# Retention scores of a pair of heads computed together, with the pass over the queries' lower parts on 64 rows of the matrix unit for each head

## The chip, the core and the metric

The kernel runs on one core of one Trainium2 chip. A core has a matrix unit (TensorE; in profiles PE, and PEld for the loading of its stationary operands), a vector engine (VectorE, DVE), a scalar engine (ScalarE, ACT), a general engine (GpSimd, POOL) and SyncE (SP), which here only issues transfers. Each engine works through its own list of instructions in order and waits on semaphores for the others. 16 DMA engines move data between the chip's memory and the on-chip buffers. The metric is the time of one execution in microseconds (us), taken as the median of several runs.

## The reference

One layer of a streaming encoder on 2048 positions of width 1024: a normalization, one wide input projection, a branch of chunked attention, a branch of retention, gates, two output projections, a merge, a last projection and a last normalization, all in 32-bit floats. The change lies in retention, whose core is this (heads H = 8, key width 64, value width 128, chunks of 64):

```python
s = jnp.einsum('bnqhd,bnkhd->bnhqk', qc, kc) * intra_decay
o_intra = jnp.einsum('bnhqk,bnkhe->bnqhe', s, vc)
kv = jnp.einsum('bnkhd,hk,bnkhe->nbhde', kc, state_decay, vc)
def step(state, kv_n):
    return state * chunk_decay[None, :, None, None] + kv_n, state
_, state_prev = lax.scan(step, jnp.zeros((B, H, dk, dv)), kv)
o_cross = jnp.einsum('bnqhd,nbhde->bnqhe', qc, state_prev) * cross_decay.T[:, :, None]
```

The scores `s` are products of queries and keys over 64 numbers, weighted with a decay.

## The kernel before

**Parts.** To reach 32-bit accuracy, operands are split into an upper part (a rounded copy, made by ScalarE) and a lower part (the rest, made by VectorE or GpSimd), and a product is the sum of the products of parts.

**Stages.** The kernel runs: first half of the positions projected, attention for it, retention for it; the same for the second half; then the merge. Retention, `retention(s, ps_ret)` for s = 0 and 1, works through the four pairs of heads `p`, and in each through four stretches of 256 positions `st` (T = 256), so 16 steps for each half and 32 in all. In each step both heads `i` = 0, 1 of the pair are taken one after the other.

**Filling.** Retention's own matmuls stand between matmuls of a projection (`ps_g_...` in the profile) that are ready at any time: `fill(n)` writes n portions of these, each of three matmuls of 512 columns, into TensorE's order. What other engines do is put off by `later(n, fn)`: `fn` is written when n more portions have been. The order in which the code is written is the order of each engine's list.

**One step before the change.** `load_scored(p, st)` brings keys and queries, written two steps ahead of their use. The tile of keys, `kr`, has 128 rows: on rows 0 to 63 the keys' upper parts for both heads, on rows 64 to 127 their lower parts; two transfers, one for each half of the rows. Each head's tile of queries, `qr`, holds the queries' upper part and, behind it, their lower part, and both once more on the other 64 rows; two transfers for each head. SyncE issues these six one after the other. `scores(p, st, i)` then makes the scores of one head in one accumulator bank (`sr`, two banks) with four matmuls on all 128 rows: for each half `kk` of the keys, the keys' 128 rows with the queries' upper part, and again with their lower part. The bank holds 256 columns for the first half of the keys and 128 for the second, where the decay is zero for the rest. Because upper and lower keys lie on different rows, each pass sums two products of parts; the second pass adds upper keys by lower queries and lower keys by lower queries.

**Behind the scores** VectorE multiplies with the decay mask (`sm`), ScalarE takes the upper part (`sh`), GpSimd the lower (`sl`). `output(p, st, i, ...)` adds, in the only bank `o`, the state's share (`o<-qr,sstk`) and the scores' share (`o<-sh,vr`, `o<-sl,vr`). `evacuate` copies `o` for both heads (ScalarE: `oz`, then the squares), sends `oz` out (SyncE, `ors<-oz`) and sums the squares (`ssq`). `update` adds to the state (`kv`).

**Order of one step.** With n counting heads, the loop writes for each: a fill, `output` of this head, `scores` of the same head of the next step, for the first head `load_scored` of the step after that, and a fill. So the scores of the two heads are half a step apart.

**Buffers.** All these tiles come from one pool of 25 equal buffers; a tile takes a buffer when an earlier one is done with, and its first writer waits for that one's last reader.

In the profile every operation is at line 143, a helper that records it; tiles are told by name.

Of the kernel before, what the change touches and what calls it, by code (L numbers as in the profile page):

```python
# [11 lines left out]
F32 = mybir.dt.float32  # L12
# [9 lines left out]
P = 128  # L22
# [8 lines left out]
T = 256  # L31
# [42 lines left out]
def hybrid_kernel(  # L74
# [30 lines left out]
    def r32(ap):  # L105
        return ap.bitcast(F32)
# [47 lines left out]
    dma = Ordered(nc.sync).dma_start  # L154
# [90 lines left out]
    def later(n, fn):  # L245

        order[0] += 1
        deferred.append((steps[0] + n, order[0], fn, free[0]))
        deferred.sort(key=lambda e: e[:2])
# [86 lines left out]
    class Strassen(Chunk):  # L336
        tag = ""
# [1274 lines left out]
    def retention(s, ps_ret):  # L1612
# [4 lines left out]
        todo = [(p, st) for p in range(4) for st in range(4 * s, 4 * s + 4)]  # L1617
        tiles, values, dms = {}, {}, {}
        begun = [False]

        def load_scored(p, st):
# [5 lines left out]
            qs = []  # L1627
            for n in range(2):
                dma(
                    r32(ks[64 * n:64 * n + 64]),  # L1630
                    r32(krscr[cc][b][un, n, 2 * (p % 2):2 * (p % 2) + 2]).rearrange("i c h t -> (c h) i t"),
                )
            for i in range(2):
# [33 lines left out]

        def scores(p, st, i):

            nm = f"{p}_{st}_{i}"  # L1670
            ks, qs = tiles[p, st]
            sp = ps_ret.tile([P, 512], F32, tag="sr", bufs=2, name=f"sr_{nm}")[:, 0:T + P]
            for kk in range(2):
                o = sp[:, kk * T:T + kk * P]
                kcol = ks[:, i, kk * P:(kk + 1) * P]
                pe.matmul(o, kcol, qs[i][:, 0, kk * P:], start=True, stop=False)
                pe.matmul(o, kcol, qs[i][:, 1, kk * P:], start=False, stop=True)
            got = []
# [14 lines left out]

            later(1, masked)
            return got
# [114 lines left out]
        fill(13)  # L1810
        parts = {items[0]: scores(*items[0])}
        fill(RET_FILL)
        parts[items[1]] = scores(*items[1])
        fill(RET_FILL * 2)
        for n, (p, st, i) in enumerate(items):
# [12 lines left out]
            if i == 1:  # L1828
                pend = evacuate(p, st, ops)
            if n + 2 < len(items):  # L1830
                parts[items[n + 2]] = scores(*items[n + 2])
            if i == 0 and m + 2 < len(todo):
                load_scored(*todo[m + 2])
            fill(RET_FILL)
            if n % 8 in (4, 6) and p < 3:
                load_mask(p + 1, n % 8 // 2 - 2)
        fill(9)
# [204 lines left out]
```

## Time and profile before

| | |
|---|---|
| median of 3 runs | 1908.64 us (1907.68 to 1913.85) |
| the profiled execution's own time | 1909.69 us |
| its span from first to last instruction | 1907.9 us |
| matmuls, loads of stationary operands | 10213 each |
| score matmuls of 256 columns, 128 columns (`sr<-qr,kr`) | 128 of each, busy 29.1 and 21.6 us |
| retention's two stretches | about 565 to 717 us and 1325 to 1480 us |
| transfers of keys and of queries for the scores | 64 of 128 KB, 128 of 128 KB |

Busy times are sums over overlapping instructions and don't add up to the time that they hold up what follows; the distance between the starts of neighbouring instructions does. A row such as `x4` in the order of time merges neighbours of the same kind; its first number is the first one's start, the second the time from there to the last one's end. A bracket at a row's end is the time in which the engine stood still before it, and what ended that. `SPq` and `ACTq` are the queues in which SyncE and ScalarE issue transfers.

### The profile page before, as it was taken

To read this page: it belongs to the slowest core of one execution; us is meant where nothing else is said; L and a number is where in the kernel's file an instruction comes from. 1 tells how busy PE (TensorE), PEld (TensorE's weight loads), DVE (VectorE), ACT (ScalarE), POOL (GpSimd) and SP (SyncE) were. 2 spreads that over 40 slices of the span, in tenths; PEclk is the share of its full clock that TensorE was granted. 3 is DMA by queue.
4 is the path that set the end of the run, shared out by engine and by line. 5 is a ranking of instruction groups with operands and counts; after the bars stand their busy time and mean duration, and the time that the engine had idled before them with its cause. 6 is when DMAs were issued, how large, how long until landed. Compare 5 with 4: busy or idle time off the path is not lost. (4 is left out here: it accounts for less than half of the span.)

```text
span 1907.9 us, 31062 instructions
## 1 busy us (share of the span) xinstructions
PE 1866.9 (98%) x10213; PEld 1604.4 (84%) x10213; DVE 1355.7 (71%) x2456; ACT 933.1 (49%) x1931; POOL 665.3 (35%) x583
## 2 busy tenths in 40 slices
PE   7999999999999999999999999999999999999998
PEld 6899889888888888899889888887888878888886
DVE  6879888677655658889798677765546766767665
ACT  7555554666654455443333666664455321223544
POOL 0102105455645561001105554554564000002775
PEclk9999999999999999999999999999999999999999
DMA  6586976666549987775776656555998999986673
GB/s 197 158 275 200 282 265 213 185 193 185 175 144 278 279 257 258 231 233 195 222 247 202 185 165 180 166 150 155 275 283 265 326 355 345 322 291 227 209 238 127
DMA packets 325553, 435.88 MB, mean 228 GB/s; under 512 B 29880, under 2 KB 191184, under 8 KB 325392
## 3 DMA queue, kind: packets, MB, share of 16 engines
q1 hardware_dynamic: 260096, 368.35, 60.7%
q10 hardware_dynamic: 65296, 65.55, 11.2%
q8 instruction: 81, 1.33, 0.3%
q14 instruction: 80, 0.66, 0.1%
HBM read 288.14 MB, written 145.64 MB: 227 GB/s over the span
## 5 line engine op out<-in xcount | busy, mean ns | idle before, releaser
L143 POOL TENSOR_SCALAR pr<-pr,rsum 128x640 f32<-128x640 f32 (+4 forms) x128 | 100.0, 781 | 197.7 <-DVE rsum L143 130.7
L143 DVE TENSOR_TENSOR ptl<-tp,pth 128x512 fp32r<-128x512 f32 (+1 forms) x168 | 100.3, 597 | 91.7 <-ACT pth L143 77.8
L143 ACT ACTIVATE pr<-pr,mn 128x640 f32<-128x640 f32 (+4 forms) x128 | 97.9, 765 | 123.3 <-DVE mn L143 97.3
L143 PE MATMUL ps_g_x<-r,wh_g 128*128 128x512 f32 x448 | 141.5, 397 | 1.0 <-ACT u_g L143 0.9
L143 PE MATMUL ps_g_z<-r,wh_g 128*128 128x512 f32 x448 | 141.1, 396 | 0.0
L143 POOL TENSOR_TENSOR l_vr<-vrt,h_vr 128x512 fp32r<-128x512 f32 x32 | 47.7, 1492 | 202.4 <-DMA qrs<-l_q 131.6
L143 POOL TENSOR_TENSOR t_out<-raw_out 128x512 f32<-128x512 f32 x7 | 14.1, 2008 | 263.2 <-DVE wl_out L143 263.2
L143 DVE CUSTOM_DVE_ANT_0 pr<-wide,bt 128x640 f32<-128x640 f32 (+4 forms) x128 | 93.7, 732 | 16.5 <-PE wide L143 13.5
L143 ACT CAST pth<-tp 128x512 fp32r<-128x512 f32 (+1 forms) x168 | 85.3, 507 | 38.9 <-PE tp L143 34.2
L143 PE MATMUL wide<-ka,qa 128*128 128x384 f32 (+1 forms) x448 | 94.9, 327 | 2.9 <-DVE mn L143 2.7
L143 DVE TENSOR_TENSOR sm<-sr,dm 128x384 f32<-128x384 f32 x64 | 35.6, 556 | 85.3 <-PE sr L143 33.9
L143 ACT CAST wh_p<-raw_p 128x512 fp32r<-128x512 f32 x111 | 67.9, 618 | 51.0 <-PE ps_p_y L143 18.2
L143 POOL TENSOR_TENSOR sl<-sm,sh 128x384 fp32r<-128x384 f32 x64 | 69.8, 1090 | 64.8 <-ACT sh L143 44.0
L143 PEld LDWEIGHTS tp<-ident,pr 128*128 128x128 f32 x560 | 71.8, 141 | 23.5 <-POOL pr L143 1.0
L143 PEld LDWEIGHTS ps_g_x<-r,wh_g 128*128 128x128 f32 x448 | 79.6, 189 | 13.9 <-ACT u_g L143 2.3
L143 PEld LDWEIGHTS ps_g_z<-r,wh_g 128*128 128x128 f32 x448 | 79.5, 188 | 12.4
L143 PE MATMUL tp<-ident,pr 128*128 128x128 f32 x560 | 89.0, 272 | 0.3
L143 PE MATMUL ps_g_z<-r,wl_g 128*128 128x512 f32 x224 | 88.2, 394 | 0.0
L143 PE MATMUL ps_g_x<-r,wl_g 128*128 128x512 f32 x224 | 88.1, 393 | 0.0
L143 POOL TENSOR_TENSOR wl_g<-t_g,wh_g 128x512 fp32r<-128x512 f32 x56 | 75.5, 1349 | 35.1 <-ACT wh_g L143 33.8
L143 DVE TENSOR_TENSOR wl_p<-raw_p,wh_p 128x512 fp32r<-128x512 f32 x111 | 79.5, 723 | 7.7 <-ACT wh_p L143 5.4
L143 POOL TENSOR_TENSOR t_g<-raw_g,t_g 128x512 f32<-128x512 f32 x56 | 73.8, 1318 | 28.1 <-issue 8.9
(927 smaller groups left out, 6016.7 us busy)
## 6 DMA issues: line engine op xcount, KB each, us to landing
raw_g<-in_w_in_dram ACTq DMA_DIRECT2D x56, 512.0 KB, 4.9
raw_p<-in_w_in_dram ACTq DMA_DIRECT2D x50, 512.0 KB, 5.8
qa<-qas SPq DMA_DIRECT2D x128, 128.0 KB, 3.4
qr<-qrs SPq DMA_DIRECT2D x128, 128.0 KB, 4.8
vr<-vrs SPq DMA_DIRECT2D x64, 256.0 KB, 5.6
ka<-kas SPq DMA_DIRECT2D x56, 256.0 KB, 4.1
va<-vas SPq DMA_DIRECT2D x40, 256.0 KB, 3.4
kds<-kdt_k SPq DMA_DIRECT2D x32, 256.0 KB, 4.8
```

The costliest lines, as they stand in the source:

```text
L143: return tc.keep_in_program_order(op(*a, **k))
```

## The change

Both heads' scores of a step are made in one place, right behind the first head's `output` of the step before; their eight matmuls come in two passes of four. In the first, each head and each half of the keys has a matmul on all 128 rows with the queries' upper part. In the second, each has one with the queries' lower part on 64 rows only: the first head on rows 0 to 63, the second on rows 64 to 127, taking turns. For that, the keys of the second head are loaded the other way round, upper parts on rows 64 to 127, so that the 64 rows used hold upper parts for both heads; the keys come in four transfers of 64 rows by 256 columns. The product of lower keys and lower queries is no longer computed. The second head's mask and split are written one portion after the first head's. Fills stay as many; the masks of the next pair's second head are loaded one head sooner.

```diff
         def load_scored(p, st):
 ...
-            for n in range(2):
-                dma(
-                    r32(ks[64 * n:64 * n + 64]),
-                    r32(krscr[cc][b][un, n, 2 * (p % 2):2 * (p % 2) + 2]).rearrange("i c h t -> (c h) i t"),
-                )
+            for i in range(2):
+                for n in range(2):
+                    at = 64 * (n ^ i)
+                    dma(
+                        r32(ks[at:at + 64, i]),
+                        r32(krscr[cc][b][un, n, 2 * (p % 2) + i]).rearrange("c h t -> (c h) t"),
+                    )
 ...
-        def scores(p, st, i):
+        def scores(p, st):
+
+            ks, qs = tiles[p, st]
+            sps = [ps_ret.tile([P, 512], F32, tag="sr", bufs=2, name=f"sr_{p}_{st}_{i}")[:, 0:T + P] for i in range(2)]
+            todo = [(sps[i][:, kk * T:T + kk * P], i, kk) for kk in range(2) for i in range(2)]
+            for o, i, kk in todo:
+                pe.matmul(o, ks[:, i, kk * P:(kk + 1) * P], qs[i][:, 0, kk * P:], start=not kk, stop=False,
+                          skip_group_check=True)
+            for o, i, kk in todo:
+                hi = slice(64 * i, 64 * i + 64)
+                pe.matmul(o, ks[hi, i, kk * P:(kk + 1) * P], qs[i][hi, 1, kk * P:], start=False, stop=bool(kk),
+                          skip_group_check=True)
+            for i in range(2):
+                parts[p, st, i] = scored(p, st, i, sps[i])
+
+        def scored(p, st, i, sp):
 
             nm = f"{p}_{st}_{i}"
-            ks, qs = tiles[p, st]
-            sp = ps_ret.tile([P, 512], F32, tag="sr", bufs=2, name=f"sr_{nm}")[:, 0:T + P]
-            for kk in range(2):
-                o = sp[:, kk * T:T + kk * P]
-                kcol = ks[:, i, kk * P:(kk + 1) * P]
-                pe.matmul(o, kcol, qs[i][:, 0, kk * P:], start=True, stop=False)
-                pe.matmul(o, kcol, qs[i][:, 1, kk * P:], start=False, stop=True)
 ...
-            later(1, masked)
+            later(1 + i, masked)
 ...
-        parts = {items[0]: scores(*items[0])}
-        fill(RET_FILL)
-        parts[items[1]] = scores(*items[1])
-        fill(RET_FILL * 2)
+        scores(*todo[0])
+        fill(RET_FILL * 3)
 ...
-            if n + 2 < len(items):
-                parts[items[n + 2]] = scores(*items[n + 2])
+            if i == 0 and m + 1 < len(todo):
+                scores(*todo[m + 1])
             if i == 0 and m + 2 < len(todo):
                 load_scored(*todo[m + 2])
             fill(RET_FILL)
-            if n % 8 in (4, 6) and p < 3:
-                load_mask(p + 1, n % 8 // 2 - 2)
+            if n % 8 in (4, 5) and p < 3:
+                load_mask(p + 1, n % 8 - 4)
```

On TensorE, at the first step of the first half (`sr_0_0` and `sr_0_1` are the two heads' banks, in the short form of the names; `qr_0_0`, `qr_0_1` their queries):

```order
 L143 MATMUL ps_g_8_y<-r_88,wl_g_8_1_7065 128x512
-L143 MATMUL sr_0_0_7181<-qr_0_0_7091,kr_0_7088 128x256 x2
-L143 MATMUL sr_0_0_7181<-qr_0_0_7091,kr_0_7088 128x128 x2
+L143 MATMUL sr_0_0_7185<-qr_0_0_7093,kr_0_7088 128x256
+L143 MATMUL sr_0_1_7186<-qr_0_1_7096,kr_0_7088 128x256
+L143 MATMUL sr_0_0_7185<-qr_0_0_7093,kr_0_7088 128x128
+L143 MATMUL sr_0_1_7186<-qr_0_1_7096,kr_0_7088 128x128
+L143 MATMUL sr_0_0_7185<-qr_0_0_7093,kr_0_7088 128x256
+L143 MATMUL sr_0_1_7186<-qr_0_1_7096,kr_0_7088 128x256
+L143 MATMUL sr_0_0_7185<-qr_0_0_7093,kr_0_7088 128x128
+L143 MATMUL sr_0_1_7186<-qr_0_1_7096,kr_0_7088 128x128
```

The head's four matmuls have become the pair's eight, the heads taking turns; the last four are those on 64 rows.

On ScalarE, around the evacuation of the output of the second step of the first pair (`sh_2_0`, `sh_2_1`: upper parts of the third step's scores, first and second head), before:

```order
L143 CAST sh_2_0_7407<-sm_2_0_7396 128x384
L143 ACTIVATE u_g_8_7287<-u_g_8_7287 128x512
L143 DMA raw_g_10_1_7411<-in_w_in_dram 128x4x256
L143 CAST wh_g_9_3_7413<-raw_g_9_1_7125 128x512
L143 COPY oz_1_7436<-o_1_7331 128x512
L143 ACTIVATE o_0_1_7437<-o_1_7331 128x512
L143 CAST o2h_1_7464<-o_0_1_7437 128x512
L143 CAST sh_2_1_7466<-sm_2_1_7440 128x384
```

and after the change:

```order
L143 CAST sh_2_0_7422<-sm_2_0_7409 128x384
L143 ACTIVATE u_g_8_7300<-u_g_8_7300 128x512
L143 DMA raw_g_10_1_7426<-in_w_in_dram 128x4x256
L143 CAST wh_g_9_3_7428<-raw_g_9_1_7129 128x512
L143 CAST sh_2_1_7446<-sm_2_1_7415 128x384
L143 COPY oz_1_7448<-o_1_7341 128x512
L143 ACTIVATE o_0_1_7449<-o_1_7341 128x512
L143 CAST o2h_1_7476<-o_0_1_7449 128x512
```

The second head's cast has moved from behind the squares' cast to the place right ahead of the output's copy.

On SyncE, the loads of the third step, before:

```order
L143 DMA vr_1_1_7238<-vrs_0_213 128x512
L143 DMA kr_2_7269<-krs_1_182 64x2x256 x2
L143 DMA qr_2_0_7272<-qrs_1_190 64x512 x2
L143 DMA qr_2_1_7275<-qrs_1_190 64x512 x2
L143 DMA mas_0_333<-g_0_2_0_7226 128x512
```

and after the change:

```order
L143 DMA vr_1_1_7242<-vrs_0_213 128x512
L143 DMA kr_2_7278<-krs_1_182 64x256 x4
L143 DMA qr_2_0_7283<-qrs_1_190 64x512 x2
L143 DMA qr_2_1_7286<-qrs_1_190 64x512 x2
L143 DMA mas_0_333<-g_0_2_0_7230 128x512
```

Two transfers of keys more stand ahead of the queries.

2 lines of the change are left out of this document (1 added, 1 removed).

## The prediction

> **What bounds the kernel now.** I read the page first, then the two stretches in which retention runs, then TensorE's order of time inside one of them.
>
> ```profile
> span 1907.9 us, 31062 instructions
> PE 1866.9 (98%) x10213; PEld 1604.4 (84%) x10213; DVE 1355.7 (71%) x2456; ACT 933.1 (49%) x1931; POOL 665.3 (35%) x583
> ...
> 565.00:717.00 152.00, 145.48 (x849) 125.41 (x848) 83.61 (x162) 73.28 (x146) 89.56 (x74) 0.99 0.92 269
> ...
> 1325.00:1480.00 155.00, 151.40 (x887) 130.89 (x887) 82.94 (x160) 78.47 (x153) 87.99 (x72) 1.00 0.93 274
> ```
>
> TensorE (PE, with its weight loads PEld) sets the end: 98% of the span. In the two retention stretches (the last two rows: busy time of PE, PEld, DVE, ACT, POOL, then clock, share of the DMA engines, GB/s) it stands still for 6.5 and 3.6 us, and the 16 DMA engines are at 0.92 and 0.93, so memory is a near second there. What the score matmuls cost is not their busy time, since matmuls overlap, but the distance from one start to the next:
>
> ```profile
> 600.12 0.39 PE L143 MATMUL ps_g_y<-r,wl_g 128*128 128x512 f32 x1
> 600.35 0.28 PE L143 MATMUL ssq<-o2h,ohr 128*32 128x256 f32 x1
> 600.47 0.28 PE L143 MATMUL ssq<-o2l,ohr 128*32 128x256 f32 x1
> ...
> 600.70 0.28 PE L143 MATMUL ssq<-o2l,ohr 128*32 128x256 f32 x1
> 600.82 0.40 PE L143 MATMUL o<-qr,sstk 128*128 128x256 f32 x2
> ...
> 601.47 0.28 PE L143 MATMUL o<-sl,vr 128*128 128x128 f32 x1
> 601.58 0.27 PE L143 MATMUL o<-sh,vr 128*128 128x128 f32 x1
> 601.69 0.62 PE L143 MATMUL sr<-qr,kr 128*128 128x256 f32 x4
> 602.15 0.68 PE L143 MATMUL ps_g_y<-r,wh_g 128*128 128x512 f32 x2
> ...
> 601.52 0.19 PEld L143 LDWEIGHTS o<-sh,vr 128*128 128x128 f32 x1
> 601.63 0.54 PEld L143 LDWEIGHTS sr<-qr,kr 128*128 128x128 f32 x4
> 602.09 0.30 PEld L143 LDWEIGHTS ps_g_y<-r,wh_g 128*128 128x128 f32 x2
> ```
>
> A matmul of 256 columns takes 0.12 us of the stream (600.35 to 600.47), and one of 128 columns 0.11, though it has half the work (601.47, 601.58, 601.69): there the weight loads set the pace, 0.11 us apart (601.52 to 601.63; 601.63 to 602.09 for four). The four score matmuls of a head take 0.46 us (601.69 to 602.15), 0.92 for a pair of heads, 29.4 us in the 32 steps.
>
> **The change part by part.** *The lower pass.* Eight matmuls a step stay eight. Four of them, the upper pass, keep all 128 rows: 2 x 0.12 + 2 x 0.11 = 0.46 us. The other four now use 64 rows each, in two couples with no row in common and different accumulators. If a couple runs at once, loads too, the lower pass takes 0.23 us in place of 0.46: 32 x 0.23 = **7.4 us less**. If nothing runs at once it takes four loads at 0.11 in place of 0.46: 0.02 x 32 = 0.6 us less. Those are the ends; no row of this trace has a matmul on 64 rows. I take 7.4: the rows of the array are loaded and fed by their own partitions, and a couple shares none of them. That is argued, not shown.
>
> The Trainium skill, TensorEngine Tiling (Array Packing), section Tiling Modes, says that different tiles load weights and multiply in parallel; by it the term is the 7.4. TensorE: Matmul & The Clock Gate, section on LDWEIGHTS, says that a load's time goes by its columns and not by its rows; by it alone, with loads one after the other, the term would be the 0.6.
>
> *The queries must be there earlier.* Both heads' scores now stand where the first head's stood, so the second head's queries are needed half a step (some 4.5 us) sooner, and nothing may pass them on TensorE: behind them stand the filling matmuls of the projection. SyncE (SPq) issues a step's transfers in order, keys, then four of queries; landing is counted from the issue:
>
> ```profile
> 564.59 2.73 SPq L143 DMA_DIRECT2D qr<-qrs  x4
> 570.87 0.64 PE L143 MATMUL sr<-qr,kr 128*128 128x256 f32 x4
> ...
> 1385.49 4.41 SPq L143 DMA_DIRECT2D qr<-qrs  x4
> 1393.09 0.62 PE L143 MATMUL sr<-qr,kr 128*128 128x256 f32 x4
> ...
> DMA to landing us min/median/max: 2.6/4.8/7.2
> ...
> 634.67 0.65 PE L143 MATMUL sr<-qr,kr 128*128 128x256 f32 x4 [0.65 <-DMA qr<-qrs]
> ```
>
> With the last of the four issued about 0.6 us ahead of the end of the group and 4.8 us to landing, the first step's last queries land at 564.59 + 2.73 - 0.6 + 4.8 = 571.5, and TensorE asked at 570.87: 0.6 us of new wait. Reckoned so, six of the 32 steps come out short, the two above being the first and the last of them (in that one the last issue came 0.4 us ahead of the end of the group: 1385.49 + 4.41 - 0.4 + 4.8 = 1394.3 against 1393.09), by 0.4 to 1.2 us, 4.6 us together. A step that waits hands its wait to the next as slack, if SyncE has run on meanwhile; if it always has, only the longest of each stretch counts, 2 x 1.2 = 2.4. I take the middle, 3.5. In two steps TensorE waited for the first head's queries already (the last row is the longer of them).
>
> *The keys' transfers* go from two to four a step, each of 64 rows and 1 KB a row:
>
> ```profile
> 615.85 1.28 SPq L143 DMA_DIRECT2D kr<-krs  x2
> 617.22 2.47 SPq L143 DMA_DIRECT2D qr<-qrs  x4
> ...
> L143 SPq DMA_DIRECT2D kr<-krs x64: 594/606/2174, 563.3 to 1465.2; - x64
> ...
> L143 SPq DMA_DIRECT2D state<-sts x4: 450/456/597, 1331.4 to 1438.8; - x4
> ```
>
> Two cost 1.3 us with what stands between them. The nearest row is the state's reload, the same 64 rows of 1 KB: 456 ns, so four take 4 x 0.5 = 2.0, 0.7 us more; at the old 606 ns they take 2.5, 1.2 more. The queries behind them on SyncE go out 0.7 to 1.2 us later. Lower end: nothing, because a landing of 4.8 us against a least one of 2.6 means 2 us of standing in line at engines that are 0.92 busy, and a later issue meets a shorter line. Upper end: all 1.2 us land later, and by the reckoning above 22 of the 32 steps are short, 20.6 us together if no wait helped the next step, 2 x 2.4 = 4.8 if each did; the middle is 13. I take +0.3 on the 3.5, near the lower end because of the 0.92: queries' waits **+3.8 us** in all.
>
> *The evacuation of the output moves up behind another cast.* On ScalarE the second head's cast (sh) now stands ahead of the copy of the output (oz), which frees the only output accumulator. That costs 0.51 us when ScalarE is late. But ScalarE is late for a reason that the same move changes:
>
> ```profile
> 593.51 0.51 ACT L143 CAST sh<-sm 128x384 fp32r<-128x384 f32 x1 [5.92 <-DMA ors<-oz]
> ...
> 594.97 0.57 ACT L143 COPY oz<-o 128x512 f32<-128x512 f32 x1
> ...
> 596.09 0.50 PE L143 MATMUL o<-qr,sstk 128*128 128x256 f32 x2 [0.90 <-ACT o L143]
> ...
> 706.12 0.51 ACT L143 CAST sh<-sm 128x384 fp32r<-128x384 f32 x1 [6.09 <-DMA ors<-oz]
> ...
> 707.54 0.59 ACT L143 COPY oz<-o 128x512 f32<-128x512 f32 x1
> ...
> 708.67 0.80 PE L143 MATMUL o<-qr,sstk 128*128 128x256 f32 x2 [2.25 <-ACT o L143]
> ...
> PE o L143 <- ACT o L143: 4.2, 4, 2.3
> ...
> PE o L143 <- ACT o L143: 1.4, 1, 1.4
> ```
>
> The first head's cast sat 6 us for a buffer that the last output's transfer still read; two more operations then stood between it and oz (593.51 to 594.97), and TensorE waited 0.90 and 2.25 us for the squares behind it. As the changed program is built, the buffer in question goes in most steps to the second head's cast, which stands right in front of oz: the operations between run ahead of the wait, and oz comes 1.46 - 0.51 = 0.9 us sooner. The waits of TensorE at this place are 4.2 and 1.4 us (the last two rows, one for each stretch); 0.9 off each of the four long ones would be 3.6, the extra cast at all five 2.6 the other way. I take **2 us less**.
>
> *At nothing:* the second head's mask and split one or two steps earlier on VectorE and GpSimd (busy 54% and 58% of the retention rows; the product that uses them comes no sooner), and the decay masks' loads, which are issued no later against their use than before.
>
> The sum, against the profiled execution's own 1909.69 us: -7.4 + 3.8 - 2 = -5.6, so 1904.1. It stands 1.05 us above the median of the runs shown, 1908.64; in the runs that is **1903**.
>
> **The rivals.** *Loads one after the other.* For it: the even 0.11 us of full loads above. Against: two loads on separate rows were never seen. Then -0.6 + 3.8 - 2 = +1.2: 1910, no change that can be told.
>
> *The array drains when it changes its division* from 128 rows to 64 and back, twice a step. It decides as soon as a drain is longer than the gain of a step, 0.23 us. A 256-column matmul lasts 0.28 us for 0.12 of the stream, so a drain costs at least 0.16 us; with a load of 0.19 that may no longer run ahead, 0.35. 64 x 0.16 = 10.2 to 64 x 0.35 = 22 us: 1909.69 + 10.2 - 5.6 = 1914 to 1926, some 1915 in the runs at the likelier low end. Against it: the sums of squares (ssq) change to 32 columns and back, and their starts, 600.12, 600.35 and 600.70, 600.82, are 0.23 and 0.12 apart, as between matmuls alike. For it: that is a division of columns, not of rows. The Trainium skill, TensorEngine Tiling (Array Packing), section Tiling Modes, states such a drain for every change of mode; the ssq rows disagree, for columns.
>
> *SyncE passes its whole delay on.* It decides once the later issue, 0.7 to 1.2 us, is more than the line at the DMA engines gives back. With 13 us of waits in place of 3.8: 1909.69 - 7.4 + 13 - 2 = 1913.3, in the runs 1912.
>
> *No new wait at all:* the queries' terms at nothing and ScalarE's at 3.6: 1898.7, in the runs 1898.
>
> **How the numbers follow.** Forecast 0.52, loads in turn 0.22, drain 0.14, SyncE 0.08, no wait 0.04. What a measurement can tell from no change is about 0.3%, 5.7 us: below 1902.9 or above 1914.4. The forecast at 1903 lies on the first of these; its own range, 1898 to 1909, comes from the waits' bounds, and I put half of it on either side. Faster: 0.26 + 0.04 + 0.01 of loads in turn = 0.31. Slower: 0.11 of the drain, 0.03 of SyncE, 0.04 of the others with bad luck at their waits = 0.18. The same: 0.51. The range 1897.5 to 1914.5 takes in the no-wait end, loads in turn, most of SyncE's case, and leaves out most of the drain.
>
> **What would show it.** The lower pass: couples of score matmuls whose starts are a few hundredths of a us apart, and 0.69 us from the first score matmul to the filling one behind, not 0.92 (loads in turn) or over 1.0 (drain). Queries: waits of PE for qr in some six steps, 3 to 5 us in all, not 13. Keys: kr issues of 0.45 to 0.6 us. ScalarE: the second head's cast as the one that waits for the output's transfer, and PE's waits for ACT in the o rows at 3 to 4 us in place of 5.6. The forecast is wrong if the couples start 0.11 us apart, if a gap opens in front of the first or behind the last 64-row matmul, or if the waits for qr pass 8 us.

## The result and the profile after

The changed kernel is slower: 1936.42 us (median of 4 runs, 1935.39 to 1938.81) against 1910.94 us for the kernel before in the same session (4 runs, 1907.68 to 1913.85), a ratio of 1.0137, with a 95% interval from 1.0117 to 1.0156. The forecast was 1903 us, the range 1897.5 to 1914.5. About 26 us were lost, nearly all in the two stretches of retention: from the first score matmul to the last sum of squares they take 176.5 and 181.0 us, 161.7 and 170.1 before.

First the page after and the same two windows as before (busy time of PE, PEld, DVE, ACT, POOL, then clock, share of the DMA engines, GB/s):

```profile
span 1934.7 us, 31187 instructions
PE 1881.5 (97%) x10213; PEld 1606.2 (83%) x10213; DVE 1355.2 (70%) x2456; ACT 933.4 (48%) x1931; POOL 662.6 (34%) x583
...
565.00:717.00 152.00, 139.06 (x772) 114.66 (x771) 77.44 (x152) 67.32 (x132) 79.44 (x68) 0.96 0.86 255
1325.00:1480.00 155.00, 148.58 (x820) 124.51 (x819) 76.10 (x138) 69.20 (x134) 82.54 (x69) 0.98 0.79 235
```

In the first window TensorE now runs 772 matmuls where it ran 849, and in the second 820 where it ran 887. It stands still for 12.9 and 6.4 us where it stood for 6.5 and 3.6. Its clock is 0.96 and 0.98 (0.99 and 1.00 before). The DMA engines, which I had called a near second at 0.92 and 0.93, are **less** busy: 0.86 and 0.79. So memory is not what became the bound.

What TensorE waits for in retention, before and then after (total us, times, longest):

```profile
PE o L143 <- ACT o L143: 5.6, 5, 2.3
PE sr L143 <- DMA qr<-qrs: 1.0, 2, 0.6
PE kv L143 <- DMA vr<-vrs: 0.7, 1, 0.7
```

```profile
PE sr L143 <- DMA qr<-qrs: 7.0, 8, 1.7
PE o L143 <- ACT o L143: 5.4, 6, 1.8
PE sr L143 <- DMA vr<-vrs: 3.1, 1, 3.1
PE sr L143 <- issue: 2.8, 5, 1.4
PE kv L143 <- DMA vr<-vrs: 2.1, 4, 1.2
```

The score matmuls (`sr`) waited 1.0 us in all; now it is 7.0 + 3.1 + 2.8 = 12.9. (A releaser is inferred. The wait of 3.1 put down to `vr` ended at 713.67 us, 0.2 us after the last of that step's queries had landed; those put down to "issue" stand ahead of score matmuls for whose queries the trace has no landing.) All the rows above together grew from 7.3 to 20.4 us, by some 13. With the rows that are not shown, some of which shrank, all of TensorE's waits in the two stretches grew from 10.8 to 22.7 us, by some 12.

The queue of SyncE and TensorE around the longest wait, and SyncE's queue around a second place, both of the changed kernel:

```profile
704.65 4.68 SPq L143 DMA_DIRECT2D qr<-qrs  x4
...
710.25 0.36 PE L143 MATMUL sr<-qr,kr 128*128 128x256 f32 x1 [1.02 <-DMA qr<-qrs]
713.67 1.49 PE L143 MATMUL sr<-qr,kr 128*128 128x256 f32 x7 [3.07 <-DMA vr<-vrs]
```

```profile
627.71 7.38 SPq L143 DMA_DIRECT2D kr<-krs  x4
635.19 2.46 SPq L143 DMA_DIRECT2D qr<-qrs  x4
```

Four issues of queries take 4.68 us there instead of some 2.4, and four of keys 7.38: SyncE stands still between two transfers of one group. By the issue records it stood 2.4 us ahead of the last of those queries, and 1.7 and 3.0 us between the keys; in the first and the last of these the transfer that ended the stand was one of the projection's weights (`raw_g`), which ScalarE issues.

As the program is built, each transfer of SyncE and of ScalarE takes one of eight semaphores in turn, and is not issued until the transfer that had this semaphore before, eight transfers back in the order of both engines, has landed. I call these the eight **places**. SyncE, which works in order, stands if the place of its next transfer is still held. The issue records show it: the last of the queries above was issued at 708.89 us, 0.02 us after the weights that held its semaphore had landed.

After a long wait TensorE is slow for a while. Windows of the changed kernel behind the waits at 600.8 and 713.67:

```profile
600.00:604.00 4.00, 3.20 (x11) 2.70 (x12) 1.44 (x3) 0.00 (x0) 3.02 (x3) 0.50 0.89 294
604.00:608.00 4.00, 4.00 (x18) 3.19 (x17) 0.00 (x0) 2.03 (x4) 1.47 (x2) 0.71 0.86 258
608.00:620.00 12.00, 12.00 (x73) 10.16 (x72) 4.82 (x11) 6.48 (x12) 7.74 (x7) 1.00 0.83 250
...
714.00:718.00 4.00, 4.00 (x14) 3.18 (x14) 1.44 (x3) 0.51 (x1) 1.11 (x1) 0.50 0.84 260
```

The granted clock is 0.50 there, and 14 matmuls take 4 us. By the clock's own records it was half for 6.8 us in each of these two places, and for 3.4 us in two more, at 1343.6 and 1374.3 us; in the kernel before for 3.4 us once. The waits around their starts were short: 1.8 and 1.4 us, 1.0 and 3.1, 1.0 and 1.2, and at 1374 a single one of 1.7. The Trainium skill, TensorE: Matmul & The Clock Gate, section on the clock gate, states two clocks, half and full, the half one after an idle stretch of some 3.4 us and until the unit has been busy for some 3.4 us. The trace agrees on the two clocks and, with 3.4 and 6.8 us, roughly on how long the half one lasts, but not on the idle stretch, for which 1.7 us were enough here. Over the two windows the lower clock costs 152 x 0.03 + 155 x 0.02 = some 8 us (an estimate, rather high, since TensorE stood still in a part of that time).

Last, the step itself. One step of the changed kernel in which TensorE did not wait (matmuls, then loads):

```profile
620.94 0.27 PE L143 MATMUL o<-sh,vr 128*128 128x128 f32 x1
621.05 1.00 PE L143 MATMUL sr<-qr,kr 128*128 128x256 f32 x8
621.98 0.73 PE L143 MATMUL ps_g_z<-r,wh_g 128*128 128x512 f32 x2
...
620.99 0.91 PEld L143 LDWEIGHTS sr<-qr,kr 128*128 128x128 f32 x8
621.97 0.30 PEld L143 LDWEIGHTS ps_g_z<-r,wh_g 128*128 128x128 f32 x2
```

From the first score matmul to the filling one behind are 0.93 us, not the forecast 0.69 and hardly other than the 0.92 of two heads before. The starts inside, worked out from the records as medians of the 32 steps, tell why. On the left the full-row matmuls, then the couples:

| kernel | start to start, ns | to the filling matmul | and to the next |
|---|---|---|---|
| changed | 174, 121, 59, **204**, 3, **220**, 3, **150** | 933 | 336 |
| both heads together, all rows full (fourth experiment) | 172, 121, 60, 109, 172, 118, 60, 109 | 920 | 284 |

The two matmuls of a couple start 3 ns apart, their loads too: they do run at once. But the way into the 64-row pass takes 204 instead of 109 ns, and the way out 150 instead of 109 with another 52 behind. The matmuls' starts smear this; those of their loads part it cleanly (medians again): 260 ns into the pass and 264 out of it, against 109 each with full rows, and 3, 105, 3 inside it against 111, 121, 118. So the pass saves 0.24 us, about what was forecast, and gives it back at its two ends, 0.15 us each: (933 + 336) - (920 + 284) = 65 ns a step, 2 us in 32.

So the sum of the loss goes: 12 us of waits, 8 of lower clock, 2 of the 64-row pass, together 22 of 26; the remaining 4 I cannot lay to a row.

### The profile page after: what moved, and what is told of

It reads as the page before. It is cut to its first block, busy times and chain, and to the rows that moved or that the text cites. A ratio compares the mean times of both kernels' runs of the same rounds, so it can differ in the third digit from the quotient of the medians.

```text
span 1934.7 us, 31187 instructions
## 1 busy us (share of the span) xinstructions
PE 1881.5 (97%) x10213; PEld 1606.2 (83%) x10213; DVE 1355.2 (70%) x2456; ACT 933.4 (48%) x1931; POOL 662.6 (34%) x583
## 5 line engine op out<-in xcount | busy, mean ns | idle before, releaser
L143 PE MATMUL ps_g_x<-r,wh_g 128*128 128x512 f32 x448 | 145.7, 407 | 1.0 <-ACT u_g L143 0.8
L143 POOL TENSOR_TENSOR wl_g<-t_g,wh_g 128x512 fp32r<-128x512 f32 x56 | 74.6, 1333 | 34.8 <-ACT wh_g L143 33.8
L143 ACT CAST wh_g<-t_g 128x512 fp32r<-128x512 f32 x112 | 68.9, 615 | 23.9 <-POOL t_g L143 9.3
```

Source lines behind the costliest of these rows:

```text
L143: return tc.keep_in_program_order(op(*a, **k))
```

## The experiments

The theories at the start: **T**, the two more transfers a step on SyncE; **E**, the second head's queries being needed half a step earlier; **D**, the change between 128 and 64 rows. Later T was split into **I** or **S** (SyncE's time of issuing against its slack), **L** (the eight places), **B** (smaller transfers being slower by themselves) and **Q** (the delay between keys and queries). Ratios are against the kernel before in the same session, with 95% intervals; 0.001 is 1.9 us.

### Two transfers of keys or four, in each order

The first: the changed kernel with keys in two transfers. A place in memory then holds the upper and the lower part of a key row next to each other, so that one transfer can step from one head's upper to the other head's lower part.

```diff
-            for i in range(2):
-                for n in range(2):
-                    at = 64 * (n ^ i)
-                    dma(r32(ks[at:at + 64, i]), r32(krscr[cc][b][un, n, 2 * (p % 2) + i])...)
+            for n in range(2):
+                first = krscr[cc][b][un, 2 * (p % 2), :, :, n]...
+                step = 32 * 2 * 2 * T + (T if n == 0 else -T)
+                ... ap=[rows, [step, 2], cols]
+                dma(r32(ks[64 * n:64 * n + 64]), r32(pair))
```

> The changed kernel, but each step's keys come in two transfers again (their place in memory is laid out so that a transfer of 64 rows can take one head's upper and the other head's lower part). Both heads together, 64-row pass kept. Theory T (two more transfers a step hold SyncE up; TensorE then waits for what lands late, and runs at half clock after the long waits): back to 1910 to 1917 us, waits of the score matmuls for queries at 1 to 3 us instead of 7, no more stretches at half clock than before. Theory E (both heads' queries are needed half a step earlier, whatever the number of transfers): stays at 1930 to 1937. Theory D (it is the change between 128 and 64 rows that costs): stays at 1930 to 1937, with few waits.

Measured: 1907.38 us, ratio 1.0006 (0.9994 to 1.0018).

The second is the kernel before with the four transfers of the diff in `load_scored`, nothing else:

> The kernel before, with the changed kernel's four transfers of keys a step and nothing else. Theory T: slower by 13 to 25 us, 1924 to 1936, with waits for queries, values or for SyncE's late issues. Theory E: no change, 1909 to 1913, since the second head's queries are still asked for half a step later. Theory D: no change, 1909 to 1913. If the two act only together (T uses up the slack that E had already cut), it lies in between, 1913 to 1920.

Measured: 1934.00 us, ratio 1.0141 (1.0119 to 1.0163).

The third and the fourth put the lower pass back on all rows, with four and with two transfers of keys:

```diff
-                hi = slice(64 * i, 64 * i + 64)
-                pe.matmul(o, ks[hi, i, kk * P:(kk + 1) * P], qs[i][hi, 1, kk * P:], ...)
+                pe.matmul(o, ks[:, i, kk * P:(kk + 1) * P], qs[i][:, 1, kk * P:], ...)
```

> The changed kernel with the lower pass on all 128 rows again (it computes the product of lower keys and lower queries too, as the kernel before did); both heads together, four transfers of keys. Theory T and theory E: about 2 us below the changed kernel, 1932 to 1936, with the same waits. Theory D: back to 1909 to 1915.

> Both heads' scores together, all 128 rows in both passes, two transfers of keys: of the change, the order alone is left. Theory T: 1907 to 1913, no slower than before. Theory E: 1924 to 1936, the second head's queries late. Theory D: 1907 to 1913.

Measured: 1934.24 us, 1.0143 (1.0120 to 1.0166), and 1906.49 us, 0.9998 (0.9985 to 1.0010).

With before and after these make a whole table:

| | keys in two transfers | keys in four |
|---|---|---|
| heads apart, full rows | 1 (before) | 1.0141 |
| heads together, full rows | 0.9998 | 1.0143 |
| heads together, 64 rows | 1.0006 | 1.0137 (the change) |

The column decides, the row does nothing that can be told. T holds, though the first and the fourth run came out a little faster than its ranges; E and D fall as causes of the loss. TensorE's waits in the second and in the fourth run:

```profile
PE o L143 <- ACT o L143: 10.1, 11, 1.9
PE kv L143 <- DMA vr<-vrs: 3.6, 6, 1.1
PE sr L143 <- DMA qr<-qrs: 1.8, 2, 1.0
```

```profile
PE sr L143 <- DMA qr<-qrs: 2.4, 6, 0.8
PE o L143 <- ACT o L143: 0.5, 2, 0.3
```

In the second, queries are hardly late, since the second head still has half a step; the same delay comes out at the output's copy (ScalarE's casts wait for the buffer that the late transfer `ors` reads, 60.4 us in the two stretches, 49.9 before) and at the values. So the loss isn't one late transfer: queries, values and outputs are late by turns. In the fourth, the waits for the output's copy are nearly gone, as the moved cast promised, and those for queries are 2.4 us.

### What of a transfer costs: SyncE's time, or the place

Four runs add something to the kernel before, behind each step's keys: semaphore instructions of SyncE, or two tiny transfers. Of the first kind there are three runs, with 12, 24 and 36. The expectations reckon with 47 ns for each instruction (0.56, 1.13 and 1.69 us); in the traces of these runs they are 59 ns apart, so the table has 0.71, 1.42 and 2.12 us.

```diff
+            for n in range(24):
+                tc.keep_in_program_order(nc.sync.sem_inc(slow))
```

```diff
+            for n in range(2):
+                dma(tiny[:, n], dmask[0, 0:1, 0:16])
```

> The kernel before, with 24 semaphore instructions of SyncE (47 ns apart in the trace of before, so 1.1 us) behind each step's transfers of keys: SyncE loses the time that the two more transfers take to issue, and no transfer is added. Theory I (the time of issuing is what the two transfers cost): slower by as much as four transfers of keys cost, 1924 to 1936 us. Theory L (the program lets eight transfers be under way, each issue waits until the one eight before has landed, and two more in a step use that up): 1905 to 1912, since SyncE stands still for over 2 us in each step anyway and can lose 1.1 us there. Theory B (transfers of 64 KB are served worse by the DMA engines): 1905 to 1912.

> The kernel before, with two transfers more in each step behind those of the keys, of one row of 64 bytes each, which nothing uses. Theory I: their issue on SyncE takes some 0.3 to 0.6 us each, so half of it or all: 1917 to 1936 us. Theory L: each holds one of the eight places until it has landed, some 2 us, as the larger ones hold it for 4 to 6; 1915 to 1930. Theory B: 1905 to 1912. Together with the run of issue time alone: both slow is I, only this one is L, neither is B.

> The kernel before with 12 semaphore instructions behind each step's keys, 0.56 us, half of the run of issue time alone. Theory S (SyncE's queue runs almost without slack: in the trace of before it stands 19.4 us in 28 steps in front of the first transfer of values' side, kd, 0.7 us a step, and stands otherwise for places and buffers; what is added beyond 0.7 us a step lengthens every step by the rest): 0.56 fits into the 0.7, so 1905 to 1911 us. Theory Q (what counts is how long after the keys' buffer came free the queries land; every delay in front of the queries costs in proportion): half of the 12 us that 24 instructions cost, 1912 to 1916.

> The kernel before with 36 semaphore instructions behind each step's keys, 1.69 us. Theory S: (1.69 - 0.74) x 32 = 30 us slower, 1933 to 1943, on one line with the 12 us of 24 instructions and a start at 0.74 us. Theory Q: in proportion, 18 us slower, 1922 to 1930.

| added in each step | SyncE's time | ratio | us |
|---|---|---|---|
| 12 instructions | 0.71 us | 1.0027 (1.0009 to 1.0045) | +5 |
| 24 instructions | 1.42 us | 1.0065 (1.0046 to 1.0084) | +12 |
| 36 instructions | 2.12 us | 1.0152 (1.0131 to 1.0173) | +29 |
| 2 tiny transfers | 2 x 0.26 us | 1.0118 (1.0084 to 1.0152) | +23 |
| 2 more of keys (second run) | 4 x 0.60 instead of 2 x 0.71 us (means) | 1.0141 | +27 |

SyncE's time alone costs, and bends: the first 0.71 us cost 5 us, the next 7, the last 17 of the 23 that 0.71 x 32 steps make. None of the three ranges for the 24 instructions held: 1921.12 us is less than theory I had put and more than L and B had. S had put a sharp start at 0.74 us a step and the full price beyond it; with the times in the table that makes nothing, 22 and 44 us, so S is wrong in both. Q had called for a straight line, 18 us at the third point, and falls. But SyncE's time isn't all: two tiny transfers take less of it than 12 instructions do (each 0.26 us, and 0.05 to the next) and cost 23 us in place of 5. What they take beside it is two of the eight places.

How full SyncE's queue is, from all its issue records between 575 and 706 and between 1333 and 1470 us:

| | steps | stood ahead of `kd` | of `kr` | of `qr` |
|---|---|---|---|---|
| before | 28 | 19.4 us | 9.9 | 26.6 |
| changed | 26 | 4.4 | 23.8 | 32.9 |

SyncE's standing ahead of `kd` (the keys for the state, needed late) is the time that a longer list uses up first: 0.7 us a step before the change, but 0.2 us or less in 16 of the 28 steps, and in the changed kernel it is as good as gone. By the semaphores that it waited for, some 16 of the 19.4 us were stands for a place, three of them behind weights (2.2, 3.6 and 4.9 us): the places bind in the kernel before already. The new standing is ahead of keys and queries.

Next, one issue fewer on SyncE, with all 15 transfers a step kept: ScalarE, which makes the output's copy, also issues its transfer.

```diff
-                put(2, orscr..., oz...)
+                later(2, lambda: act.dma_start(orscr..., oz...))
```

> The changed kernel, but the transfer of the output (ors) is issued by ScalarE, which makes it, instead of SyncE: the same 15 transfers with the same eight places, one issue less for SyncE a step (0.40 us and what it stands in front of it, 0.1 to 0.2). Theory S: 0.5 x 32 = 16 us off the changed kernel's 1936, 1915 to 1926. Theory L alone (places): 1930 to 1937. Theory Q: the queries go out no sooner after their keys, 1930 to 1937.

Measured: 1928.27 us, ratio 1.0110 (1.0091 to 1.0129), so 5 us off the changed kernel where S had 16 and L none; the intervals of the two ratios touch. Inconclusive between them, and S overpriced it.

### Fewer transfers

To take transfers away I first let one transfer write a head's queries to both halves of the rows, reading its source twice, alone and with four transfers of keys:

```diff
-                for half in range(2):
-                    dma(r32(q[64 * half:64 * half + 64]), rows)
+                both = bass.AP(..., ap=[[0, 2]] + rows.ap)
+                dma(r32(q)..., both)
```

> The kernel before, with a head's queries in one transfer that writes both halves of the rows, so two transfers a step instead of four; same bytes. Theories I and L: SyncE gets 1 to 1.5 us a step back and two places less are used; the transfers now seldom set anything, but in retention TensorE waited only some 3 us for transfers, so 1900 to 1908. If its issue takes as long as two transfers' did (over 1 us), no change under I. Theory B: no change, 1905 to 1909.

> The kernel before with keys in four transfers and queries in two: as many transfers as before. Theories I and L: 1903 to 1912, nothing left of the 1.014 that four transfers of keys cost with four of queries. Theory B: still slow, 1924 to 1936.

Measured: 2129.04 us, 1.1151 (1.1118 to 1.1184), and 2135.67 us, 1.1188 (1.1149 to 1.1227). Both miss, and for a reason of their own. A window of the first, 600 to 640 us in 40 slices, and its waits:

```profile
DMA  5876982111411593377598411115111198899921
GB/s 204 256 198 176 314 284 92 51 51 49 162 49 51 160 335 95 122 245 247 204 328 321 142 54 54 51 48 163 47 49 51 53 276 258 268 258 352 361 103 52
...
PE sr L143 <- DMA qr<-qrs: 88.7, 33, 6.1
```

For long stretches the DMA engines are a tenth busy, and move 50 GB/s, a fifth of the rate before. A tenth is about two engines of 16, and the transfer's outermost count is two. The Trainium skill, DMA: Bandwidth & Descriptors, section Rules for kernel authors, states that a leading broadcast of c copies confines a transfer to at most c engines; the trace agrees. These two runs say nothing on the theories, and B was not tested by them.

The second way puts both heads' queries of a step into one tile, as the keys are: two transfers of 64 rows over all engines. (Of the 25 tiles of the pool counted above, 22 are the general buffers and three smaller ones hold the state and its parts; three tiles of twice the width take the room of six of the 22.)

```diff
-                q = E(f"qr_{nm}_{i}", F32R, (P, 2, T))
+            q = epool[0].tile([P, 2, 2, T], F32R, tag="qr", bufs=3, name=f"qr_{nm}")
+            for half in range(2):
+                dma(r32(q[64 * half:64 * half + 64])..., r32(qrscr[cc][b][un, 2 * (p % 2):2 * (p % 2) + 2])...)
...
-E_RET = 22
+E_RET = 16
```

> The kernel before, but both heads' queries of a step lie in one tile of twice the width (three such tiles, in place of six of the 22 buffers of the pool), so that a transfer of 64 rows takes both heads: two transfers of 256 KB a step instead of four of 128 KB, each over all DMA engines. If SyncE's work per transfer and the eight places still bind in the kernel before (theory I and L, at thirteen transfers a step): faster, 1895 to 1903 us, with fewer waits for transfers. If they bind only beyond thirteen: 1904 to 1910. If 256 KB in one transfer land later, or three fixed tiles are too few: slower, 1912 to 1920, with waits for queries.

> The changed kernel, four transfers of keys and all, with the queries merged in the same way: thirteen transfers a step, as many as before. Theories I and L: most of the loss is gone, 1903 to 1915 us. Theory B (it is the small transfers of keys): 1925 to 1936.

> The changed kernel with keys in two transfers and queries merged: eleven transfers a step, 64-row pass kept. If transfers bind at thirteen too: faster than both, 1893 to 1903 us. If not: 1904 to 1911, like the changed kernel with keys in two transfers.

> The changed kernel with keys in two transfers and queries merged (eleven transfers, 1909.7 us; SyncE stands 1.7 us a step in front of kd), with 24 semaphore instructions, 1.13 us, between the keys and the queries. Theory S: they fit into the 1.7 us, 1907 to 1913. Theory Q: the queries land 1.1 us later where TensorE already waited for them in five steps, and it loses what the same kernel with four transfers of keys lost, 1918 to 1928.

| | transfers a step | ratio |
|---|---|---|
| before, queries merged | 11 | 0.9982 (0.9972 to 0.9991) |
| changed, keys in two, queries merged | 11 | 1.0001 (0.9990 to 1.0012) |
| the same, and 24 semaphore instructions | 11 | 1.0006 (0.9989 to 1.0024) |
| changed (keys in four), queries merged | 13 | 1.0073 (1.0049 to 1.0097) |

The kernel before with queries merged took 1904.76 us and the changed one with eleven transfers 1909.74: both lie where they were expected if transfers bind only beyond thirteen, the first 3 us faster even so. With eleven transfers, SyncE stands 1.7 us a step ahead of `kd`, mostly for buffers, and 24 semaphore instructions between keys and queries cost nothing that can be told: the same dose cost 12 us in the kernel before. That fits S, and it is the end of Q. Two more transfers of keys in place of the instructions, for no more of SyncE's time (some 1.2 us against 1.4), cost 13 us. There SyncE stands ahead of `kd` as long as in the kernel before, 18.6 us in 26 steps, and for buffers in nearly all of the longer stands: that loss isn't SyncE's time. At 1924.54 us this run misses the 1903 to 1915 that I and L had and lies at the edge of B's 1925 to 1936; but its keys of 64 KB landed no later than those of 128 KB in the run with eleven transfers (medians 4.8 and 5.0 us). SyncE's queue and TensorE in that last run:

```profile
623.56 8.85 SPq L143 DMA_DIRECT2D kr<-krs  x4
632.46 1.25 SPq L143 DMA_DIRECT2D qr<-qrs  x2
...
637.21 1.06 PE L143 MATMUL sr<-qr,kr 128*128 128x256 f32 x8 [2.12 <-DMA qr<-qrs]
```

Between the first and the second of the four keys SyncE stood 5.2 us. Its own place was the one that a transfer of weights held, which ScalarE had issued at 621.66. With two transfers in place of four, weights stood in the way of the queries for 3.1 us at that place instead, and TensorE waited 0.40 us.

### The places freed

In the last pair the weights that ScalarE issues in retention are issued by GpSimd, whose transfers have semaphores of their own. SyncE's list stays word for word.

```diff
-            (dma if self.job.resident else act.dma_start)(raw, ...)
+            (dma if self.job.resident else (pool if in_ret[0] else act).dma_start)(raw, ...)
```

> The changed kernel, but in the retention stretches the projection's weights (raw_g, 512 KB each, which ScalarE issues and which hold two to three of the eight places for 7 to 10 us each) are issued by GpSimd, whose transfers have semaphores of their own: SyncE's transfers are as many and are issued in the same time, but the eight places are theirs alone. Theory L beside S (of the 27 us, some 12 are SyncE's time of issuing and some 15 the places): the 15 are gone or more, 1912 to 1922 us, and nowhere does SyncE stand behind raw_g any more. Theory S alone: 1930 to 1937. If GpSimd's issuing holds up its own subtractions: PE waits for sl or o2l, in both runs of this pair.

> The kernel before with the same move of raw_g to GpSimd, to read the other run against. In the trace of before SyncE stood eleven times behind raw_g, 25 us in all, but mostly ahead of transfers that were not urgent. Theory L: 1900 to 1908, a little faster or the same, and the changed kernel with the same move no more than 14 us above it. Theory S alone: the changed kernel stays 25 to 27 us above it. If GpSimd's issuing costs: slower, 1910 to 1925.

Measured: the changed kernel 1921.94 us, 1.0077 (1.0057 to 1.0097); the kernel before 1901.27 us, **0.9970** (0.9956 to 0.9983). What SyncE waited for in 565 to 717 us, first in the changed kernel, then in the run of it with weights by GpSimd:

```profile
SPq L143 <- DMA vr<-vrs: 8.0, 14, 2.1
SPq L143 <- DMA raw_g<-in_w_in_dram: 7.7, 4, 3.0
SPq L143 <- DMA kd<-kds: 4.1, 6, 1.7
```

```profile
SPq L143 <- DMA kr<-krs: 4.9, 4, 1.5
SPq L143 <- DMA vr<-vrs: 3.7, 10, 0.9
```

The weights are gone from the list, and 11 us from the changed kernel's time, with nothing altered on SyncE: L is shown to be a part. It isn't all of what L had said: the kernel before gained 6 us by the same move, so the change still costs 1.0077 / 0.9970, some 20 us, where L beside S had at most 14. SyncE's own fifteen transfers share the eight places still.

### The price of a change of division

The last one changes between 128 and 64 rows twice as often, with keys in two transfers:

```diff
-            for o, i, kk in todo:
-                pe.matmul(o, ks[:, i, kk * P:(kk + 1) * P], qs[i][:, 0, kk * P:], ...)
-            for o, i, kk in todo:
-                hi = slice(64 * i, 64 * i + 64)
-                pe.matmul(o, ks[hi, i, kk * P:(kk + 1) * P], qs[i][hi, 1, kk * P:], ...)
+            for half in (todo[0:2], todo[2:4]):
+                for o, i, kk in half:
+                    pe.matmul(o, ks[:, i, kk * P:(kk + 1) * P], qs[i][:, 0, kk * P:], ...)
+                for o, i, kk in half:
+                    hi = slice(64 * i, 64 * i + 64)
+                    pe.matmul(o, ks[hi, i, kk * P:(kk + 1) * P], qs[i][hi, 1, kk * P:], ...)
```

> The changed kernel with keys in two transfers, its eight score matmuls in another order: for the first half of the keys the two matmuls on 128 rows and then the couple on 64, and the same for the second half. So a step changes from 128 rows to 64 and back twice instead of once; nothing else differs. If each change costs some 0.15 us, as the starts in the trace of the changed kernel say: 2 x 0.15 x 32 = 9.6 us above the 1907.4 of the changed kernel with keys in two transfers, 1914 to 1919. If the gaps seen there were only the loads of new operands, which the other order has too: 1905 to 1911.

Measured: 1913.58 us, ratio 1.0031 (1.0020 to 1.0042), just below the range for 0.15 us and above the other: 5 us above the 1.0006 of the same kernel with one couple of changes, not 9.6. In its trace a step reads so:

```profile
625.78 1.39 PE L143 MATMUL sr<-qr,kr 128*128 128x256 f32 x8
627.10 0.73 PE L143 MATMUL ps_g_z<-r,wh_g 128*128 128x512 f32 x2
```

Here 1.32 us lie from the first score matmul to the filling one, 0.39 more than the 0.93 above (medians of 32 steps: 1319 and 931 ns). Each of the two more changes costs 0.19 us on TensorE, 12 us in 32 steps. (By the starts of the loads, a change takes some 0.20 us longer than the 0.11 to 0.12 of full rows where matmuls of 256 columns stand ahead of it, and some 0.15 behind ones of 128, as in the changed kernel.) The time grew by less than half of that: a TensorE that needs longer for a step gives SyncE longer too, and waits less (for queries 1.5 us instead of 3.1, for the output's copy under 0.5 instead of 3.6).

## Why the prediction was wrong

**The step that failed: the keys' transfers.** The prediction counted 0.7 to 1.2 us of later issue for each step, took nearly none of it as late landing "near the lower end because of the 0.92", and put +3.8 us for all waits for queries. The runs show +27 us for the two transfers alone (second run against before). The premise held: queries did meet a shorter line. Their landing fell from 4.8 to 3.3 us in the median:

```profile
L143 SPq DMA_DIRECT2D qr<-qrs x128: 444/531/1333, 565.1 to 1497.8; - x128
...
DMA to landing us min/median/max: 2.4/3.3/7.0
...
L143 SPq DMA_DIRECT2D kr<-krs x128: 444/587/1562, 562.7 to 1495.0; - x128
```

(The row of landings is that of the queries.) But the line that mattered was not at the DMA engines. It was SyncE's own list, with the places that it stands for. The prediction looked at one transfer (when do these queries land against their use?) and never asked whether SyncE can finish a step's list in the 9.6 us that a step lasts (268 us for the 28 steps in the table above). It can only just: it has 0.7 us a step to spare ahead of `kd`, and the change takes up all of it. Beyond that a delay isn't passed on once but in every step, whatever waits for it. The prediction's sentence on waits, "A step that waits hands its wait to the next as slack, if SyncE has run on meanwhile", fails in its condition: in the changed kernel SyncE, standing itself, had not run on.

**The rival that SyncE passes its whole delay on** named the right place and the wrong mechanism: its 13 us were queries landing later by the whole delay, with the condition that the DMA engines' line gives nothing back. The line gave back more than 1 us, and the loss was twice the 13. The places were not in the prediction at all, though in the trace of before SyncE already stood behind ScalarE's weights, as this row of its queue's waits shows (565 to 717 us):

```profile
SPq L143 <- DMA raw_g<-in_w_in_dram: 13.8, 6, 4.8
```

**How the 27 us divide** is settled in part. The two transfers take SyncE some 1.1 us a step (4 x 0.60 less 2 x 0.71, and 0.05 between one and the next). Without transfers 0.71 us cost 5 us and 1.42 us 12, so that SyncE's time is some 9 of the 27, an estimate. Two places at no more of SyncE's time cost 13 us (1.0073 against 1.0006), and the two tiny transfers cost 17 more than 12 semaphore instructions, which take a little longer. So SyncE's time is about a third and the places the larger part; 9 and 13 to 17 come near the 27, but that the parts simply add up is not shown. That the places are the rest is read from differences between runs and on the pair with GpSimd, which gave back 11 us of the changed kernel, but also 6 of the kernel before. That small transfers are slower by themselves (B) was not tested on its own; that the keys' landing fell (5.7 us in the median before, 5.0 after) speaks against it.

**The lower pass: mechanism right, term mis-sized.** Couples run at once, loads too, 3 ns apart. Of the two pages of the Trainium skill weighed there, the one on tiling was right. But -7.4 us was +2: the changes of division cost 0.15 us each in the changed kernel (0.985 instead of 0.69 us a step, where 0.985 is the 0.933 and the 0.052 behind it), 0.19 in the run with four. The drain rival priced them at 0.16 or more, 10.2 us in 64 changes; measured are 9 to 12. I gave it 0.14, because the sums of squares change to 32 columns and back at no cost; columns were no evidence for rows. The Trainium skill, TensorEngine Tiling (Array Packing), section Tiling Modes, which states a drain for each change of mode, is borne out for rows. One of my signs for telling them apart was bad, too: 0.93 us lay next to the 0.92 that I had put down for loads in turn. The other held: the gap ahead of the first 64-row matmul and the one behind the last, together with the couples' starts, told the gain and the drain apart.

**The queries half a step sooner: right in kind, priced too high.** In the fourth run, where only the order moved, waits for queries were 2.4 us in six places, 1.4 more than before. I had 3.5 more, in six steps.

**ScalarE: right in direction, hidden in the change.** Forecast were 2 us less of TensorE's 5.6 us behind the output's copy. With two transfers of keys it fell to 0.5 and 3.6 us; in the changed kernel it stayed at 5.4. There ScalarE's casts waited 42.8 us for the late transfer of the output, which reads the buffer that they need; with two transfers of keys (first run) they waited 36.2. In the time of the fourth run nothing of it can be told (0.9998).

**Missed altogether:** the half clock behind waits of 1 to 3 us. It added some 8 us to 12 us of waits, more than half again.

Summed anew by what was measured: +2 for the pass, +27 for two more transfers with all that follows, nothing that can be told for the order: 1909.69 + 29 = 1938.7 against 1936.53 of the profiled execution.

## What to carry to other kernels

Before adding a transfer, add up the issuing engine's list for one step, the time that each issue takes and that it stands for a semaphore, against the step's length; if what is left is less than the new issue, as here, steps get longer, even at DMA engines that are less busy than before. Add up the places in the same way: SyncE and ScalarE, which take semaphores from one ring of eight here, waited for each other's largest transfers, so one large stream was better issued from an engine with semaphores of its own. In this kernel that alone gave 0.9970, the best of all runs here, and merging two transfers of queries into one 0.9982. Work on part of the matrix unit's rows pays when the pass is long against its two changes of division, 0.15 to 0.19 us each here.

## What the runs showed of the hardware that I had not expected

- Two matmuls on separate halves of the rows started 3 ns apart, and so did their loads. A change between 128 and 64 rows cost 0.15 to 0.19 us (some 0.20 behind matmuls of 256 columns), while no such gap stands at the change to 32 columns (starts 0.23 and 0.12 us apart in the prediction's rows).
- A transfer of one row of 64 bytes took SyncE 0.26 us to issue, and one of 64 rows and 64 KB 0.59: the number of issues weighed more than the bytes.
- A transfer with an outermost count of two left the DMA engines a tenth busy.
- One wait of 1.7 us, or two of 1.0 and 1.2 us close together, was enough to halve TensorE's clock for 3.4 us; after waits of 1.0 and 3.1 us it stayed half for 6.8.
- GpSimd issued a transfer of 512 KB in 0.77 us, where ScalarE took 0.37; though 57 to 59% of its time in retention was taken already (in the kernel before), the move paid. The row of these transfers in the kernel before with weights by GpSimd:

```profile
L143 POOL DMA_DIRECT2D raw_g<-in_w_in_dram x17: 766/766/941, 561.2 to 1401.0; - x17
```
